# Issuing the fallback path's DMAs from GpSimd in place of SyncE, in a fused ReGLU MLP

## The chip, the cores and the metric

The kernel runs on one core of one Trainium2 chip. The metric is the device time of one execution in microseconds (us). "Ratio" always means the mean time of one kernel's fast runs over the mean time of the other kernel's fast runs measured beside them, without the profiled run, so it is not quite the ratio of the medians that are quoted beside it. A run counts as fast when it is at most 1.5% above the fastest of the same kernel; all timed runs here were fast, and the one run that was looked at only once counts as of unknown state.

## The reference

```python
batch, seq, dim, hidden = 16, 256, 512, 2048
# x: (16, 256, 512), w1: (512, 4096), w2: (2048, 512), all drawn from a normal distribution, float32
def reference(x, w1, w2):
    h = x @ w1
    gate, value = np.split(h, 2, axis=-1)
    h = np.maximum(gate, 0) * value
    return (h @ w2).astype(np.float32)
```

## The kernel before

The kernel holds two ways of computing the result. The fast way works in float16 with fewer products (a Strassen scheme), and while it runs it checks that the inputs' sizes allow this. The check ends in one number, `flag`. If the flag is set, a general way computes everything again in float32. For the inputs the flag is never set: the general way is in the program, but none of its instructions runs.

```python
def tile_reglu_mlp_kernel(ctx, tc, x, w1, w2, out):
    ...
    with ExitStack() as fast:
        unfit = fast_way(fast, tc, x2, w1, w2, out2, flag)
    with tc.If(unfit > 0, label="general"):
        with ExitStack() as general:
            general_way(general, tc, x2, w1, w2, out2)

def general_way(ctx, tc, x2, w1, w2, out2):
    ...
    for k in range(NK):
        for j in range(0, 2 * H, 1024):
            t = xp.tile([P, 1024], F32, name="g_t", tag="g_t")
            nc.sync.dma_start(out=t, in_=w1[k * P:(k + 1) * P, j:j + 1024])
            nc.vector.tensor_copy(out=w1_sb[:, k, j:j + 1024], in_=t)
    ...                      # 16 loads of w1, 16 of w2, 32 of x, 32 stores: 96 DMAs, all from SyncE

# in the fast way: the last output of all
        def P4(self):
            nc.scalar.activation(self.o[:, 1, :DO // 2], self.Y, COPY, scale=1 / GS)
            self.send(1, slice(0, DO // 2 if self.end else DO))       # SyncE issues it
# ... and the flag, read into a register of each of the five engines 11 to 19 us before the end
            job(78, lambda: verdict.append(nc.values_load(flag[0:1, 0:1], ...)))
            job(84, lambda: tc.mark_branch_hint_location("general", "LikelyTaken", [ENG.PE, ENG.DVE, ENG.SP]))
```

What the author doesn't write, the framework adds. Every DMA from SyncE adds 16 to one of eight semaphores ("lanes"), in turn; DMAs from GpSimd have eight lanes of their own. (To issue a DMA is to hand a transfer to the DMA engines; it has landed when its last part of 16 has been counted.) At the very end SyncE waits until all lanes and all engines' counters stand at their final values. A final value must be the same whichever arm of the `If` ran. So the empty arm has to raise every lane by what the general way would have added, and it may do that only when the lane's own last DMA has landed. This is SyncE's built program after its last output DMA, which is on lane 7:

```
branch on the register
empty arm:  8 x   wait until lane i >= 208, then add 192 to lane i          (i = 0 ... 7)
end:        3 x   wait for two GpSimd lanes each
            8 x   wait until lane i >= 400 (and for one engine's counter)   (i = 0 ... 7)
            drain, drain, barrier, GpSimd clears the semaphores, barrier
```

## Time and profile before

Six runs gave a median of 309.47 us (308.88 to 310.2); the first three of them gave 309.0 us. The first lines below are from the page of the profiled execution: each engine's busy time with its share of the span, and the chain of work that ended last.

```profile
span 307.5 us, 5285 instructions
...
PE 300.7 (98%) x1905; PEld 184.0 (60%) x1905; DVE 235.9 (77%) x388; ACT 176.4 (57%) x348; POOL 151.4 (49%) x189
...
## 4 chain that ended last, share of the span: by engine, by line
PE 96%; DMA 1%; SPq 0%; POOL 0%; ACT 0%; issue 0%
```

TensorE (PE) is busy for 98% of the span and makes up 96% of the chain. A change elsewhere can help only at the two ends. The end is where this one acts. Next come lines of three views of the same execution: SyncE's timeline (start in us, duration in us, what), the view of the source line of the `If` (L42), and that of the end of the program (L785). "SPq" is SyncE's sequencer; the three numbers before the times are the least, median and largest duration in ns.

```profile
303.38 1.07 SPq L370 DMA_DIRECT2D out_dram<-o  x1
```

```profile
L42 SPq EVENT_SEMAPHORE  x8: 17/17/17, 305.0 to 305.8; - x8
...
L42 SPq COMPARE_BRANCH  x1: 73/73/73, 304.5 to 304.5; - x1
```

```profile
L785 SPq EVENT_SEMAPHORE  x13: 17/28/28, 305.9 to 307.4; - x13
```

They read as a queue in order: the last output is issued from 303.38 on, SyncE branches at 304.5, eight semaphore instructions of the empty arm run from 305.0 to 305.8, and only after the eighth do the end waits begin. (Eleven of the 13 instructions on L785 are the end waits; the last two belong to the barriers.) With one digit more, from the records of the single instructions and of the DMA's semaphore updates:

| event | us |
|---|---|
| ScalarE's last eviction (the copy of the last result out of TensorE's accumulator) ends | 303.353 |
| SyncE issues the last output | 303.379 to 304.451 |
| SyncE branches | 304.502 to 304.575 |
| adds on lanes 0 to 6 | 305.030 to 305.522 |
| last part of the last output lands | 305.814 |
| add on lane 7 | 305.831 |
| eleven end waits | 305.897 to 306.544 |
| end of the span | 307.461 |

From the landing to the end it is 1.647 us. The last issue takes 1.07 us although most output issues take 0.33, and after SyncE's branch 0.455 us pass before its next record.

### The profile page before, as it was taken

How to read it: one execution, taken by the hardware profiler on the slowest of the kernel's cores; microseconds unless marked ns; L12 is line 12 of the kernel's file. 1: busy time of each engine (PE TensorE's matmuls, PEld its weight loads, DVE VectorE, ACT ScalarE, POOL GpSimd, SP SyncE). 2: the span in 40 equal slices, each digit the busy share in tenths (PEclk: the TensorE clock that was granted, in tenths of full speed). 3: DMA queues.
4: the chain of work that ended last, by engine and by line, in shares of the span. 5: the costliest groups of instructions: out<-in, count | busy, mean ns of one | idle time of the engine just before them, and what ended most of it. 6: DMA issues, size and time to landing. Idle time of an engine off the chain costs nothing.

```text
span 307.5 us, 5285 instructions
## 1 busy us (share of the span) xinstructions
PE 300.7 (98%) x1905; PEld 184.0 (60%) x1905; DVE 235.9 (77%) x388; ACT 176.4 (57%) x348; POOL 151.4 (49%) x189
## 2 busy tenths in 40 slices
PE   7999999999999999999999999999999999999994
PEld 6844444588844444478864444458884444448883
DVE  2579888899768888887438888889536888888841
ACT  2488886455865555538845555546865555553231
POOL 2389999800069899200029889700007998700000
PEclk9999999999999999999999999999999999999998
DMA  6976779964765260001354910000335110001132
GB/s 207 357 257 190 227 177 174 225 123 87 270 193 86 69 136 3 0 0 67 136 175 103 207 34 2 0 2 24 115 108 167 35 34 0 3 1 34 53 120 74
DMA packets 35837, 32.88 MB, mean 107 GB/s; under 512 B 14432, under 2 KB 31328, under 8 KB 35680
## 3 DMA queue, kind: packets, MB, share of 16 engines
q1 hardware_dynamic: 33536, 26.22, 28.0%
q0 software_dynamic: 2272, 6.29, 11.4%
q8 instruction: 16, 0.26, 0.4%
q14 instruction: 13, 0.11, 0.1%
HBM read 27.26 MB, written 12.58 MB: 130 GB/s over the span
## 4 chain that ended last, share of the span: by engine, by line
PE 96%; DMA 1%; SPq 0%; POOL 0%; ACT 0%; issue 0%
PE Y L250 26%; PE X L250 17%; PE W L250 17%; PE Y L362 14%; PE X L362 9%; PE W L362 9%; DMA w_stage<-in_w_dram 1%; PE X L325 1%; PE W L325 1%; PE Y L325 1%; PE Y L498 0%; PE X L498 0%; SPq L488 0%; PE Y L154 0%; POOL w_B L466 0%; ACT o L405 0%
## 5 line engine op out<-in xcount | busy, mean ns | idle before, releaser
L250 PEld LDWEIGHTS <-w_T 128*128 128x128 f16 x496 | 48.3, 98 | 57.3 <-POOL w_T L232 1.1
L179 POOL TENSOR_TENSOR fold<-xh 128x1024 f32<-128x1024 f16 x16 | 30.3, 1894 | 94.5 <-DMA xh<-x 93.7
L250 PE MATMUL X<-x_A,w_B 128*128 128x512 f16 x248 | 73.8, 379 | 0.0
L250 PE MATMUL Y<-x_S,w_T 128*128 128x512 f16 x220 | 65.5, 379 | 0.0
L250 PEld LDWEIGHTS <-w_B 128*128 128x128 f16 x372 | 36.4, 98 | 42.0
L277 DVE SCALAR_TENSOR_TENSOR cc<-W,pu 128x512 f32<-128x512 f32 x62 | 42.9, 691 | 21.2 <-ACT pu L271 20.4
L257 ACT COPY Y<-X 128x512 f32<-128x512 f32 x62 | 35.4, 571 | 38.2 <-PE X L250 37.9
L271 ACT ACTIVATE pu<-Y 128x512 f32<-128x512 f32 x62 | 37.1, 598 | 33.9 <-PE Y L250 32.9
L182 POOL TENSOR_TENSOR fold<-fold 128x512 f32<-128x512 f32 (+2 forms) x96 | 51.8, 539 | 7.5
L362 PEld LDWEIGHTS <-w_stage 128*128 128x128 f16 x512 | 50.0, 98 | 5.8
L287 DVE SCALAR_TENSOR_TENSOR cc<-Y,pu 128x512 f32<-128x512 f32 x62 | 42.9, 691 | 6.7
L282 DVE SCALAR_TENSOR_TENSOR g<-X,cc 128x512 f16<-128x512 f32 x62 | 42.8, 691 | 2.3
L299 DVE SCALAR_TENSOR_TENSOR g<-Y,cc 128x512 f16<-128x512 f32 x62 | 42.2, 681 | 1.8 <-PE Y L250 1.8
L362 PEld LDWEIGHTS <-g 128*128 128x128 f16 x384 | 37.6, 98 | 8.2
L264 ACT ACTIVATE pu<-W 128x512 f32<-128x512 f32 x62 | 37.2, 600 | 0.8 <-PE W L250 0.6
L250 PE MATMUL W<-x_S,w_B 128*128 128x512 f16 x124 | 36.9, 379 | 0.0
L250 PE MATMUL W<-x_S,w_T 128*128 128x512 f16 x124 | 36.9, 379 | 0.0
L250 PE MATMUL Y<-x_A,w_T 128*128 128x512 f16 x124 | 36.9, 379 | 0.0
L362 PE MATMUL X<-w,g 128*128 128x256 f16 x256 | 31.9, 273 | 0.0
L394 DVE SCALAR_TENSOR_TENSOR o<-W,pu 128x256 f32<-128x256 f32 x16 | 6.8, 422 | 19.8 <-PE W L362 19.8
L169 DVE TENSOR_TENSOR w_stage<-g 128x1024 f16<-128x1024 f16 x32 | 21.4, 683 | 0.2
L232 POOL TENSOR_TENSOR w_T<-w_stage 128x512 f16<-128x512 f32 (+1 forms) x16 | 18.7, 1177 | 2.5 <-DMA w_stage<-in_w_dram 2.5
(100 smaller groups left out, 306.2 us busy)
## 6 DMA issues: line engine op xcount, KB each, us to landing
w_stage<-in_w_dram SPq DMA_DIRECT2D x14, 512.0 KB, 6.2
out_dram<-o SPq DMA_DIRECT2D x26, 256.0 KB, 2.1
x<-in_x_dram POOLq DMA_DIRECT2D x4, 1024.0 KB, 9.0
xh<-x SPq DMA_DIRECT2D x16, 256.0 KB, 3.0
w<-in_w_dram POOLq DMA_DIRECT2D x2, 1024.0 KB, 10.2
out_dram<-o SPq DMA_DIRECT2D x12, 128.0 KB, 1.7
w_stage<-in_w_dram SPq DMA_DIRECT2D x4, 256.0 KB, 5.4
x_S<-in_x_dram SPq DMA_DIRECT2D x4, 256.0 KB, 6.1
```

The lines of the kernel that those rows point to most:

```text
L169: eng.tensor_tensor(o[n], o[i0], o[i1], op=op)
L179: nc.gpsimd.tensor_tensor(fold, t, t, op=MULT)
L182: nc.gpsimd.tensor_tensor(fold[:, :, :m], fold[:, :, :m], fold[:, :, m:2 * m], op=ADD)
L250: nc.tensor.matmul(ps, wop[wn][:, b, self.jb * P:(self.jb + 1) * P], self.xo[xn][:, b, :], start=fresh and b == 0, stop=b == 1, skip_group ...
L257: nc.scalar.copy(out=self.Y, in_=self.X)
L264: nc.scalar.activation(self.p5, self.W, COPY, scale=GS)
L271: nc.scalar.activation(self.u2, self.Y, COPY, scale=GS)
L277: nc.vector.scalar_tensor_tensor(out=self.c12, in0=self.W, scalar=GS, in1=self.u2, op0=MULT, op1=ADD)
L282: nc.vector.scalar_tensor_tensor(out=self.g[:, self.jb, :TH], in0=self.X, scalar=0.0, in1=self.c12, op0=MAX, op1=MULT)
L287: nc.vector.scalar_tensor_tensor(out=self.c22, in0=self.Y, scalar=GS, in1=self.p5, op0=MULT, op1=ADD)
L299: nc.vector.scalar_tensor_tensor(out=self.g[:, self.jb, TH:], in0=self.Y, scalar=0.0, in1=self.c22, op0=MAX, op1=MULT)
L362: nc.tensor.matmul(ps, self.op[an][:, i], vop[wn][:, i], start=name in ("P1", "P5") and i == 0, stop=i == NJ // 2 - 1, skip_group_check=True)
```

## The change

The general way issues its DMAs from GpSimd. The intent is in the change's own words: no SyncE lane has then to be balanced between the two arms.

```diff
@@ general_way: all four DMA lines (loads of w1, w2, x; store of the output)
-            nc.sync.dma_start(out=t, in_=w1[k * P:(k + 1) * P, j:j + 1024])
+            nc.gpsimd.dma_start(out=t, in_=w1[k * P:(k + 1) * P, j:j + 1024])
 ...
-            nc.sync.dma_start(out=out2[c * TH + b * P:c * TH + (b + 1) * P, :], in_=o)
+            nc.gpsimd.dma_start(out=out2[c * TH + b * P:c * TH + (b + 1) * P, :], in_=o)
```

In the built program, the instructions of all five engines up to the branch are the same, waits included. SyncE's empty arm has nothing left to do. GpSimd's empty arm gets four waits for GpSimd lanes and one increment of the eight of them, which waits too (the view of L42 below counts five waits, because one was there before). There are twelve end waits, since all eight GpSimd lanes are used now.

More of the change, by code (lines that the diff above doesn't have):

```diff
@@ L66, in general_way @@
         t = xp.tile([P, DO], F32, name="g_t", tag="g_t")
-        nc.sync.dma_start(out=t, in_=w2[h * P:(h + 1) * P, :])
+        nc.gpsimd.dma_start(out=t, in_=w2[h * P:(h + 1) * P, :])
         nc.vector.tensor_copy(out=w2_sb[:, h], in_=t)
@@ L72, in general_way @@
             t = xp.tile([P, D], F32, name="g_t", tag="g_t")
-            nc.sync.dma_start(out=t, in_=x2[c * TH + b * P:c * TH + (b + 1) * P, :])
+            nc.gpsimd.dma_start(out=t, in_=x2[c * TH + b * P:c * TH + (b + 1) * P, :])
             for k in range(NK):
```

## The prediction

> **What bounds the kernel.** TensorE: the page gives PE 98% busy at clock 0.996, and the chain that ended last is 96% PE, up to 302.95 of the 307.46 us span. The general way does not run for this input: none of its instructions is in the trace. So the change acts only after the flag's test, in the last 3 us. Up to the branch, all engines' instruction order is unchanged.
>
> **The tail before, from the instruction records of the last 5 us.** The last ScalarE eviction ends at 303.35. SyncE issues the last output DMA at 303.379 (1.07 us; most issues take 0.33), branches at 304.502 (73 ns) and has its next record at 305.030: the empty arm, eight waits-and-adds, one for each SyncE lane, that raise it by the 192 counts which the general way would have added. Seven take 80 ns each (305.03 to 305.52); the eighth waits for the last DMA, landed at 305.814, and runs at 305.831. Then come eleven end waits, 62 ns each (305.897 to 306.544), two drains, barrier, semaphore clear, second barrier; the span ends at 307.46, 0.945 us after the last end wait began.
>
> **What the change removes and adds.**
> - SyncE: the eight adds go, so the end waits start right after the branch. They are twelve now. Eleven ask for what is long done: started between 304.65 and 305.0, they are over by 305.35 to 305.7, behind the flight of the last DMA. The twelfth passes with its landing, about 305.83.
> - So ten end waits leave the chain: landing, one wait, the same 0.945 us. Estimate: end at 306.78, 0.68 us earlier.
> - SyncE's branch goes over one instruction in place of about 190. The Trainium skill ("Runtime: NRT & Kernel Launch", Instruction fetch mechanics) says that a taken branch to a target outside the fetched window forces a fetch. The trace agrees in kind: 0.455 us from SyncE's branch to its next record, 0.13 us on ScalarE, whose general arm is empty. This 0.3 us helps only what is hidden.
> - GpSimd: five waits and one increment of software DMA semaphores are added, and its branch gets longer. It branches at 289.48 and is needed at 306.68; 2 us is hidden.
> - PE, DVE, ACT: unchanged.
>
> **Prediction.** 309.0 − 0.7 = 308.3 us, range 307.5 to 309.2. Chances: faster by over 2% 0.01, within 2% 0.98, slower by over 2% 0.01.
>
> **What would show each step right.**
> - Instruction records: no SyncE adds after its branch; first end wait within 0.2 us of the branch's end; eleven over before the last landing, the twelfth within 30 ns of it; from landing to the end of the span about 0.96 us, where it was 1.65.
> - Page: PE's busy time, the chain and the DMA counts unchanged; a few more GpSimd instructions, all near 290 us.
> - The landing stays near 305.8 if the 1.07 us issue stays. It ran beside two instruction fetches (16 KB from 303.06, 8 KB from 303.60), which look like PE's and SyncE's.
>
> **What would make it wrong.** If the 8 KB fetch belongs to SyncE's far jump and slows the last issue, it may vanish: up to 0.7 us more (307.6). If SyncE has to stop for a fetch within its end waits, part of the gain is lost. 0.2% is near the spread of single runs (308.88 to 310.2), so the medians may hide it. Over 2 us would mean that something before the branch moved.

## The result, and the profile after

| | before | after |
|---|---|---|
| median of 6 runs, us | 309.47 (308.88 to 310.2) | 308.38 (307.95 to 309.21) |
| ratio, 95% interval | | 0.997 [0.995, 0.999] |
| span of the profiled run, us | 307.461 | 307.156 |

In a later set of five rounds the changed kernel gave 308.44 us against 309.2 us, ratio 0.9983 [0.9968, 0.9997]. So the gain is 0.2 to 0.3%, some 0.5 to 0.9 us. By the rule of 2% this is "the same"; the intervals exclude no gain at all.

These are the lines of the changed kernel's profile that answer to the ones above, from the page, from SyncE's timeline, and from the views of L42 and L785 (POOL is GpSimd).

```profile
span 307.2 us, 5283 instructions
...
PE 301.6 (98%) x1905; PEld 184.2 (60%) x1905; DVE 236.0 (77%) x388; ACT 176.3 (57%) x348; POOL 151.2 (49%) x189
...
PE 96%; DMA 2%; SPq 1%; issue 0%; ACT 0%
```

```profile
303.48 1.34 SPq L370 DMA_DIRECT2D out_dram<-o  x1
```

```profile
L42 POOLq EVENT_SEMAPHORE  x5: 17/43/43, 290.1 to 290.4; - x5
...
L42 POOLq INC_SWDGE_SEM  x1: 316/316/316, 290.5 to 290.5; - x1
...
L42 SPq COMPARE_BRANCH  x1: 68/68/68, 304.9 to 304.9; - x1
```

```profile
L785 SPq EVENT_SEMAPHORE  x14: 17/28/28, 305.1 to 307.1; - x14
```

The eight SyncE instructions on L42 are gone, and the end waits begin 0.137 us after the branch. GpSimd's new work (1.2 us from the end of its branch to the end of the increment) is over at 290.8, 14 us before SyncE's first end wait asks for it (305.08). The waits of SyncE (engine and line that waited, for what, total us, times, longest) show the same thing from the other side, first before the change, then after it, both from 303 us on:

```profile
SPq L42 <- SPq L42: 0.8, 2, 0.5
SPq L785 <- PEq L785: 0.7, 2, 0.5
```

```profile
SPq L785 <- PEq L785: 0.7, 2, 0.5
SPq L785 <- DMA out_dram<-o: 0.4, 1, 0.4
```

Before, SyncE waited on L42 (the empty arm); the profile puts these two waits down to SyncE itself, but the second of them (305.522 to 305.831 in the records) ended with the landing at 305.814. After, the one wait for the output DMA is an end wait, the twelfth and last one: it passes at 306.210, 0.017 us after the landing at 306.193. The eleven others were over at 305.746. From the landing to the end it is 0.963 us, 0.684 less than before.

The profiled span fell by 0.305 us only, because the landing came later: ScalarE's last eviction ended 0.098 us later, and the last issue took 1.344 us in place of 1.072. That second number isn't the change's doing, as the experiments show; it moves from run to run.

### The profile page after: what moved, and what is told of

Its sections match the earlier page's. It is cut to its first block, busy times and chain, and to the rows that moved or that the text cites. A ratio compares the mean times of both kernels' runs of the same rounds, so it can differ in the third digit from the quotient of the medians.

```text
span 307.2 us, 5283 instructions
## 1 busy us (share of the span) xinstructions
PE 301.6 (98%) x1905; PEld 184.2 (60%) x1905; DVE 236.0 (77%) x388; ACT 176.3 (57%) x348; POOL 151.2 (49%) x189
## 2 busy tenths in 40 slices
DMA packets 35836, 32.87 MB, mean 107 GB/s; under 512 B 14432, under 2 KB 31328, under 8 KB 35680
## 4 chain that ended last, share of the span: by engine, by line
PE 96%; DMA 2%; SPq 1%; issue 0%; ACT 0%
PE Y L250 26%; PE X L250 17%; PE W L250 17%; PE Y L362 14%; PE W L362 9%; PE X L362 9%; DMA x_A<-in_x_dram 2%; PE X L325 1%; PE W L325 1%; PE Y L325 1%; PE Y L498 0%; PE X L498 0%; SPq L217 0%; SPq L488 0%; ACT o L405 0%
```

## The experiments

ScalarE's last eviction ends anywhere from 302.6 to 303.5 us in the profiled runs, with the same program before it. This spread is as large as the effects. So the table measures each run's profile from there: the last output's issue, its flight from the end of the issue to the last landing, and the stretch from the landing to the end. Together with some 0.03 us before the issue they make up the tail. Each row rests on one profile, but the stretch from the landing to the end repeats closely: it is 0.963 or 0.964 us in all eight profiles in which SyncE has a branch and no adds, and 1.647 in both with the full adds of the kernel before. All in us; median and ratio as above.

| run | last issue | flight | landing to end | tail | median | ratio to the kernel before |
|---|---|---|---|---|---|---|
| before | 1.072 | 1.363 | 1.647 | 4.108 | 309.47 | 1 |
| changed kernel | 1.344 | 1.371 | 0.963 | 3.705 | 308.38 | 0.997 [0.995, 0.999] |
| e1: 8 loads on SyncE | 1.215 | 1.372 | 1.710 | 4.322 | 309.51 | 1.002 [0.9998, 1.0042] |
| e2: 7 loads on SyncE | 1.376 | 1.365 | 1.381 | 4.148 | 308.95 | 0.9996 [0.998, 1.0013] |
| e3: far jump | 0.992 | 1.378 | 0.963 | 3.358 | 308.31 | 0.9979 [0.9962, 0.9995] |
| e4: no general way | 0.332 | 1.359 | 0.958 | 2.674 | 307.65 | 0.9961 [0.9943, 0.9979] |
| e5: late branch | 0.333 | 1.369 | 0.964 | 2.692 | 307.62 | 0.995 [0.9933, 0.9966] |
| e6: late PE only | 0.332 | 1.598 | 0.963 | 2.918 | 307.79 | 0.9964 [0.9942, 0.9985] |
| e7: late DVE only | 1.038 | 2.119 | 0.964 | 4.146 | one look | |
| e8: ScalarE sends | 0.376 | 2.236 | 0.964 | 3.606 | 308.37 | 0.9976 [0.9953, 0.9999] |
| e9: before, late branch | 0.332 | 1.365 | 1.647 | 3.369 | 308.33 | 0.9974 [0.9961, 0.9987] |
| e10: changed kernel again | 1.210 | 1.369 | 0.964 | 3.568 | 308.44 | 0.9983 [0.9968, 0.9997] |
| e11: late branch again | 0.332 | 1.365 | 0.964 | 2.686 | 307.72 | 0.9957 [0.9944, 0.997] |

The runs e1 to e4 shared one set of runs of the kernel before (308.84 us), e5 to e8 another (309.06), e9 to e11 a third (309.2). All results were correct.

### Is it the adds, or the shorter program?

The change does two things to SyncE: it takes the eight adds out of the empty arm, and it shortens SyncE's program, so that the branch no longer jumps over some 190 instructions. Theory A says that the add on lane 7 is the cost: it waits for the last landing and stands, in order, in front of all end waits. Rival B says that the long jump is the cost.

**e1** puts eight loads of the general way back on SyncE, one for each lane.

```diff
-            nc.gpsimd.dma_start(out=t, in_=w1[k * P:(k + 1) * P, j:j + 1024])
+            eng = nc.sync if k * 4 + j // 1024 < 8 else nc.gpsimd
+            eng.dma_start(out=t, in_=w1[k * P:(k + 1) * P, j:j + 1024])
```

> The changed kernel, with the first 8 loads of the general way back on SyncE: one for each of its eight lanes, so the empty arm has eight adds of 16 again, among them the add on lane 7, which the last output DMA uses. SyncE's jump stays short (about 25 instructions). Theory A (an add on the lane of the last DMA stands in order before the end waits and holds all twelve back until the landing): no gain; from the last landing to the end of the span 1.71 us (1.65 as before, one end wait of 0.06 more), time near the kernel before (ratio 0.998 to 1.002). Rival B (the gain comes from the shorter SyncE program and jump): landing to end 0.96 us and ratio about 0.997.

The views of L42 and of the program's end, in e1:

```profile
L42 SPq EVENT_SEMAPHORE  x8: 17/17/17, 305.1 to 305.9; - x8
```

```profile
L786 SPq EVENT_SEMAPHORE  x14: 17/28/28, 306.0 to 307.5; - x14
```

The stretch from the landing to the end is 1.710 us, as Theory A had it to the last digit, and the gain in time is gone (ratio 1.002). But the test was less clean than planned. After SyncE's branch 0.455 us pass before the next record, as in the kernel before, not 0.137 as after the change; in that sense 25 instructions were already a long jump. So e1 alone doesn't refute Rival B.

**e2** has seven loads there, so only the add on lane 7 goes (`< 7` in the same line).

> As the run before, but 7 loads on SyncE: the empty arm has seven adds, on lanes 0 to 6, none on lane 7. One DMA less than the run before, in an arm that never runs. Theory A: seven adds (0.08 us each) and eleven end waits (0.062 us each) can run while the last DMA flies; they need 1.25 us from SyncE's branch, and the landing comes about 1.3 us after it, so landing to end is 0.96 to 1.2 us: 0.5 to 0.75 less than with eight. Rival B: the same as with eight, to 0.06 us.

The same two views, in e2:

```profile
L42 SPq EVENT_SEMAPHORE  x7: 17/17/17, 305.0 to 305.4; - x7
```

```profile
L786 SPq EVENT_SEMAPHORE  x14: 17/28/28, 305.5 to 307.1; - x14
```

The end waits start at 305.494, before the landing at 305.738; in e1 they started after it. One DMA less, in an arm that never runs, takes 0.329 us out of the stretch after the landing. It did not reach the expected 0.96 to 1.2 us, and the miss is arithmetic: I had counted with a gap of 0.14 us after the branch, and it was 0.456. The branch ended at 304.496; 0.456 of gap, seven adds in 0.54 and eleven end waits in 0.68 us take SyncE to 306.17. So the twelfth wait came 0.435 us after the landing: now SyncE's own queue was the last to finish. In time e2 can't be told from the kernel before (0.9996, with 1 inside the interval), so what it shows is in its trace alone.

**e3** leaves SyncE without adds, but makes its program as long as before, with 190 drains (a sequencer instruction, filler here) in the arm that never runs.

```diff
     make_identity(nc, ident)
+    for _ in range(190):
+        nc.sync.drain()
```

> The changed kernel, with 190 drains put into SyncE's general arm, which never run: no adds in the empty arm, but SyncE's program is as long and its jump as far as before the change. Theory A: landing to end stays at 0.96 us; after the branch there is a gap of some 0.45 us (0.14 with the short jump), hidden behind the landing up to about 0.2 us of it at most not. Rival B: the gain goes, landing to end near 1.65 us, ratio about 1.000.

The same two views, in e3, where SyncE has only its branch on L42:

```profile
L42 SPq COMPARE_BRANCH  x1: 73/73/73, 304.5 to 304.5; - x1
```

```profile
L787 SPq EVENT_SEMAPHORE  x14: 17/28/28, 305.0 to 306.7; - x14
```

The jump is far again (gap 0.455 us, and the branch takes 73 ns as before the change, not 68), and the gain stays whole: 0.963 us from the landing to the end, ratio 0.9979. Rival B falls. The far jump does cost 0.32 us, but on an engine that then waits for the landing anyway.

### What makes the last issue slow?

With the adds gone, the tail still has an issue of 1.0 to 1.4 us where 0.33 is usual. In both first traces a 16 KB instruction fetch of PE overlaps it. PE branches at 301.79 (before), jumps far, and 0.77 us after the branch's end a fetch begins. These are DMA records, on queue 8 for PE and queue 14 for the other engines (start and end, in us; e7 and e10 came later):

| run | PE's fetch (16 KB) | last issue | issue's end after the fetch's |
|---|---|---|---|
| before | 303.057 to 304.071 | 303.379 to 304.451 | 0.380 |
| changed kernel | 303.151 to 304.442 | 303.478 to 304.822 | 0.380 |
| e1 | 302.962 to 304.128 | 303.294 to 304.509 | 0.381 |
| e2 | 302.666 to 303.992 | 302.997 to 304.373 | 0.381 |
| e3 | 303.148 to 304.139 | 303.467 to 304.459 | 0.320 |
| e7 | 302.943 to 303.938 | 303.273 to 304.311 | 0.373 |
| e10 | 302.544 to 303.708 | 302.879 to 304.089 | 0.381 |

In six of the seven the issue ends 0.37 to 0.38 us after the fetch does; in e3 0.32. That pointed to Theory C, that PE's fetch holds up the issue, against Rival D, that the last issue is slow for a reason of its own.

**e4** leaves the general way out (right for these inputs only), and with it the branch and the jumps.

```diff
-    with tc.If(unfit > 0, label="general"):
-        with ExitStack() as general:
-            general_way(general, tc, x2, w1, w2, out2)
...
-            job(84, lambda: tc.mark_branch_hint_location("general", "LikelyTaken", [ENG.PE, ENG.DVE, ENG.SP]))
```

> The changed kernel without the general way, the branch and its hints (right for these inputs only): a floor, and a test of what slows the last output's issue. In both traces the 16 KB instruction fetch of PE that begins 0.8 us after PE's branch overlaps that issue, and the issue ends 0.38 us after the fetch. Theory C (PE's fetch holds the issue up): without the jump there is no such fetch, the last issue takes 0.33 us and its landing comes 0.7 to 1.0 us earlier; with that the span falls by about 0.8 us against the changed kernel (ratio to the kernel before about 0.994). Rival D (the last issue is slow for a reason of its own): it still takes over 1 us.

SyncE's timeline and its waits in e4:

```profile
303.16 0.33 SPq L367 DMA_DIRECT2D out_dram<-o  x1
```

```profile
SPq L781 <- DMA out_dram<-o: 0.7, 1, 0.7
```

There is no fetch after 299.43 us, and the last issue takes 0.332 us. The tail is 1.03 us shorter than the changed kernel's. The ratio is 0.9961 where about 0.994 was expected, and its interval, [0.9943, 0.9979], just misses that. But e4 takes away too much to name the cause, hence the next runs.

**e5** keeps everything and only moves the fetches: PE and DVE must wait for a ScalarE copy after the last eviction before they branch. The result of the read isn't used; the framework keeps of it a plain wait on ScalarE's counter.

```diff
         prev = stream
+    late = wpool.tile([1, 1], dt.int32, name="late")
+    nc.scalar.copy(out=late, in_=flag)
+    nc.values_load(late[0:1, 0:1], engines=(ENG.PE, ENG.DVE), min_val=0, max_val=1,
+                   skip_runtime_bounds_check_because="a copy of the flag")
     return verdict[-1]
```

> The changed kernel, with PE and DVE kept from their branches until ScalarE has copied the flag after its last eviction, so that the instruction fetches which follow their jumps (about 0.8 us after PE's, 1.4 us after DVE's) begin near 304.9 us in place of 303.1 and 303.7, when the last output has nearly landed. Theory C (a fetch that runs beside the last issue holds it up): the last issue takes 0.33 us, its landing comes about 1.4 us after the end of the issue, near 304.9, and the span is about 0.6 to 1.2 us shorter than that of the changed kernel (ratio to the kernel before 0.993 to 0.996). Rival D (the issue is slow for a reason of its own): it still takes over 0.9 us, and the ratio stays near 0.997 to 0.998.

From e5, SyncE's timeline and the view of L42:

```profile
303.15 0.33 SPq L370 DMA_DIRECT2D out_dram<-o  x1
```

```profile
L42 DVEq COMPARE_BRANCH  x1: 90/90/90, 303.3 to 303.3; - x1
L42 PEldq COMPARE_BRANCH  x1: 497/497/497, 303.4 to 303.4; - x1
L42 SPq COMPARE_BRANCH  x1: 68/68/68, 303.5 to 303.5; - x1
```

PE and DVE now branch at 303.4 and 303.3, 1.5 and 1.1 us later than in the changed kernel. Their fetches begin at 304.614 and 304.744, somewhat earlier than I expected, but still after the last output's data had been moved (its last packet ended at 304.506). The last issue takes 0.333 us, and the tail is 2.692 us: that of e4, with the general way in place. Rival D falls. The ratio is 0.995 [0.9933, 0.9966], and 0.9957 [0.9944, 0.997] when the run was repeated.

**e6 and e7** hold back only PE (`engines=(ENG.PE,)`) or only DVE (`engines=(ENG.DVE,)`).

> As the run before, but only PE waits; DVE jumps early, and its 8 KB fetch falls into the last issue. If it is PE's 16 KB fetch that holds the issue up: 0.33 us again, but one of the 16 parts of the last or the last but one output may land up to 1 us late, so the gain may be partly lost. If any fetch does: about 0.8 us of issue (the 8 KB fetch ends near 304.05, and 0.38 us more).

> As that, but only DVE waits; PE's 16 KB fetch falls into the last issue as in the changed kernel. Theory C with PE's fetch as the cause: the issue takes 1.0 to 1.35 us and ends 0.38 us after that fetch; of the last but one output only one of 16 parts lands late, not two. If DVE's fetch is the cause: 0.33 us.

The last issue in e6 and in e7, from SyncE's timelines:

```profile
302.99 0.33 SPq L370 DMA_DIRECT2D out_dram<-o  x1
```

```profile
303.27 1.04 SPq L370 DMA_DIRECT2D out_dram<-o  x1
```

In e7 PE's fetch (302.943 to 303.938) alone gives an issue of 1.038 us, and one part of the last but one output is late, not two, as expected; so PE's fetch is enough. In e6 DVE's fetch (303.082 to 303.609) alone leaves it at 0.332; but it began 0.1 us after the issue did, so this doesn't show that an 8 KB fetch could never do harm. What each fetch does to a transfer is plain in the landings of the single parts. An output lands in 16 parts, which normally arrive within 0.2 us. The parts of the last but one output and the last one:

| run | fetches beside it | last but one output | last output |
|---|---|---|---|
| changed kernel | PE's and DVE's | 14 by 304.35; 305.21, 305.63 | 16 from 306.01 to 306.19 |
| e5 | none | 16 by 304.02 | 16 from 304.68 to 304.86 |
| e6 | DVE's (303.08), PE's (304.47) | 15 by 303.86; 304.61 | 15 by 304.68; 304.92 |
| e7 | PE's (302.94), DVE's (304.99) | 15 by 304.14; 305.11 | 15 by 305.69; 306.43 |

Each fetch that ran while an output's packets moved made one of its 16 parts late, by 0.2 to 1.3 us against the slowest of the others. (In e6 PE's fetch began only 0.01 us before the last data packet ended, so the late part of the last output is more likely DVE's doing.) The same happens far from the end: in all 13 traces PE's fetches near 153, 219 and 298 us also left one part of an output late, by 0.8 to 1.7 us. A fetch is one DMA record, and one part in sixteen is one DMA engine's share. The Trainium skill ("DMA: Bandwidth & Descriptors", Queues, rings and completion order) says that a queue has a ring on each of 16 engines, and that each engine takes turns between the rings it has work for. The records fit: in the changed kernel all packets of the last but one output had started by 303.99 but for 18, two shares of nine, which ran from 304.111 to 305.15, as DVE's fetch (to 304.115) and PE's (to 304.442) ended; and the DMA counts as landed only with its last part. The records kept here don't name the engine of a packet, so that the late shares sit on the fetches' engines is inferred.

**e8** lets ScalarE issue the last output in place of SyncE.

```diff
-            self.send(1, slice(0, DO // 2 if self.end else DO))
+            self.send(1, slice(0, DO // 2 if self.end else DO), nc.scalar if self.end and self.t == 3 else nc.sync)
...
-        def send(self, h, c):
-            nc.sync.dma_start(out=out_v[self.s, h, self.t, :, c], in_=self.o[:, h, c])
+        def send(self, h, c, eng=nc.sync):
+            eng.dma_start(out=out_v[self.s, h, self.t, :, c], in_=self.o[:, h, c])
```

> The changed kernel, with the very last output issued by ScalarE, which made its data, in place of SyncE. If PE's fetch holds up any issue through the shared DMA engines: ScalarE's issue also ends about 0.38 us after the fetch, and the span does not change by more than 0.2 us. If the hold-up is one of SyncE's own sequencer or queue: ScalarE's issue takes about 0.33 us, and the landing comes 0.7 us or more earlier.

ScalarE's timeline and the list of DMA issues (count, KB, us from issue to landing) in e8:

```profile
303.32 0.38 ACTq L370 DMA_DIRECT2D out_dram<-o  x1
```

```profile
out_dram<-o ACTq DMA_DIRECT2D x1, 128.0 KB, 2.6
```

Neither alternative was right as a whole. The issue takes 0.376 us, though PE's fetch (302.983 to 304.431) runs all through it: a fetch does not hold up every issue beside it. Yet little is won, since two of the 16 parts still land late (305.43 and 305.94; the other 14 by 305.04), and the flight is 2.236 us. So the faster issue alone brought nothing: the tail of 3.606 us lies between those of the changed kernel's two profiles (3.705 and 3.568). The Trainium skill says in the same page (Issuing engines are not separate DMA queues) that using several issuing engines saves only the time of the issue; this run agrees so far as only the issue got shorter, and even of these 0.97 us 0.87 were lost again in the flight, against the changed kernel's first profile.

Why SyncE's issue is held and ScalarE's isn't stays open. SyncE still had its last but one output in flight, with a part stuck behind the fetch; ScalarE had nothing. Much fits "an issue waits while SyncE's own previous DMA is stuck behind the fetch": over the 13 traces SyncE issued 20 outputs while a fetch of PE was running, and 19 of them took 0.72 to 1.41 us and ended 0.32 to 0.38 us after the fetch, each with an earlier output of SyncE's in flight that had a late part. In the kernel before, the output at 299.013, beside the fetch of 298.371 to 299.652, took 1.018 us. In e4, which has no branch at all, one at 298.794 took 1.012, so it needs no jump, only a fetch of PE. But two observations speak against the rule as it stands. The twentieth output, in e1 at 298.927, took 0.333 us, although the output before it (issued at 298.054) was in flight and had one part that landed only at 301.317, 1.2 us after the others; that issue began 0.034 us after its fetch (298.893 to 299.825), the held ones at least 0.32 us. And in the kernel before, a load issued at 36.804, inside PE's fetch of 36.172 to 37.297, took 0.367 us with an earlier load of SyncE's still in flight; only the next one was held. No run took one condition away by itself, so the reason is not shown.

### Are the two costs separate?

**e9** puts the late branch of e5 on the kernel before; **e10** and **e11** repeat the changed kernel and e5 beside it.

> The kernel before, with PE's and DVE's branches held until after the last eviction as in the run of the late branch. If the two costs are separate, only the landing moves: last issue 0.33 us, landing about 1.37 us after its end, but landing to end 1.65 us as before the change (the add on lane 7 is in front of the end waits again); span about 306.5 us, 0.68 us over the late branch on top of the change; ratio to the kernel before about 0.997.

> The changed kernel itself, to have it in the same rounds as its two neighbours: landing to end 0.96 us, last issue 1.0 to 1.35 us, ratio 0.997 to 0.998.

> The late branch on top of the change, in the same rounds as the changed kernel: landing to end 0.96 us, last issue 0.33 us, span 0.6 to 1.2 us under the changed kernel's, ratio to the kernel before 0.993 to 0.996.

SyncE's lines in e9, from its timeline and the view of L42:

```profile
303.10 0.33 SPq L370 DMA_DIRECT2D out_dram<-o  x1
```

```profile
L42 SPq EVENT_SEMAPHORE  x8: 17/17/17, 304.0 to 304.8; - x8
```

The last issue is short, and the adds cost as before: 1.647 us from the landing to the end. The tails are 3.369 (e9) and 2.686 us (e11), and the difference of 0.683 us is what the change is worth with the fetches out of the way; with them in the way it was 1.647 − 0.963 = 0.684. The costs are separate and add up. In time, the change alone, the late branch alone and both together give the ratios 0.9983, 0.9974 and 0.9957, so the two savings of 0.17% and 0.26% sum to 0.43%, which is what both give. That the sum is exact is luck, for each ratio is known only to some 0.13%; it is the tails that show the sum.

The best kernel is therefore the changed one with the late branch (e5, e11): 307.62 and 307.72 us, 0.43 to 0.5% under the kernel before. Its interval in the last set, [0.9944, 0.997], touches that of the changed kernel, [0.9968, 0.9997], only at its edge; its tail is 0.9 to 1.0 us shorter. The margin is thin: the first fetch began 0.108 us after the last output's last data packet had ended in e5, but only 0.008 us after it in e11.

## Why the prediction was right

- **Where the change acts.** Right. All instructions up to the branch are the same, PE's share of the chain stays at 96%, the DMA packets at 35,837 and 35,836, and all of the gain is after the landing of the last output.
- **The size.** Right: 0.68 us from the landing to the end was worked out, 0.684 measured, and e1, e3 and e9 took it away, kept it, and found it again on another base. Predicted 308.3 us, measured 308.38. This closeness is partly luck: the kernel before came out at 309.0 in the first runs and at 309.47 in all six, so the measured difference is 1.09 us, and 0.76 in the later set. The tail, not the medians, confirms the 0.68.
- **The mechanism.** Right: no adds after the branch, the first end wait 0.137 us after the branch's end (under 0.2 expected), eleven waits over 0.45 us before the landing, the twelfth within 0.02 us of it.
- **The shorter jump helps only what is hidden.** Right, and e3 shows it. e2 shows the limit: with seven adds left, the longer gap did come out into the open.
- **GpSimd's new work is hidden.** Right: 1.2 us near 290 us, from four new waits, where five were forecast, and the increment.
- **The landing stays near 305.8 if the 1.07 us issue stays.** Half right. The issue stayed slow, but its length follows PE's fetch (0.99 to 1.38 us in these runs), so it was 1.34 us and the landing came at 306.19. This took 0.27 us from the profiled gain.
- **Whose the fetches are.** PE's was named rightly. The 8 KB fetch "from 303.60" was said to look like SyncE's; it is DVE's. It moves with DVE's branch in e5 and e7 (to 304.74 and 304.99), stays in e6, and is there in the changed kernel, whose SyncE jumps short. The fetch that SyncE's far jump caused is a later one, at 305.58 before; it is missing after the change and is back in e3 at 305.59, and it delayed nothing.

What stays open: no run used inputs for which the general way runs, so what the change does to that way's own time is not known. Nor is it shown why the last eviction's end moves by up to 0.9 us between profiles (by 0.6 us between the two of the changed kernel), or why a fetch of PE holds up an issue of SyncE's and not one of ScalarE's.

## What to carry to other kernels

Code that never runs can cost time where it is joined to the code that does: look at what each arm of a branch must do to leave the semaphores equal, and keep any such step that has to wait for the last transfer out of the last engine's queue, or on an engine that is done early. The last output of a kernel is also a bad moment for other engines to jump far (here it cost 0.9 to 1.0 us): hold their jumps back until the data has moved, with a wait that cost nothing here because these engines were idle by then. When effects are a fraction of a percent, measure the stretch of the trace in which they act, from one fixed event to the next, and use the medians only to check the sum.

## What the Trainium skill lacked or had wrong

- "Runtime: NRT & Kernel Launch" (Instruction fetch mechanics) says that a taken branch to a target outside the fetched window forces a fetch before execution goes on, and calls the cost of crossing a block mostly hidden. These runs agree with a cost on the engine itself (SyncE's gap after a far jump is 0.455 us against 0.137), but the larger cost is on others, which the page lacks: a 16 KB fetch of PE held up SyncE's last issue by 0.7 to 1.0 us, and each fetch that ran while an output's packets moved made one of its 16 parts 0.2 to 1.7 us late. In the kernel before, on PE and SyncE, a recorded fetch came 0.77 and 1.0 us after the far jump's end, when the first instructions at the target had already run.
- The same section gives refill blocks of 16 KiB. In these traces PE's fetches are 16,384 bytes, but those of the other engines are 8,192; whether that is a setting of the runtime or a property of the chip, the runs can't tell.
- "DMA: Bandwidth & Descriptors" (Issuing engines are not separate DMA queues) does not say that an issue itself can be held up by other traffic, and differently by engine: beside PE's fetch, SyncE's last issue took 0.99 to 1.38 us and ScalarE's 0.376.
- "Advanced Engine Details and Errata" (Control Flow Timing) gives about 108 ns for a compare-and-branch. Here it took 45 ns on GpSimd, 50 to 54 on ScalarE, 68 to 73 on SyncE, 90 on DVE, and 408 to 501 on PE.
- No page tells what an empty arm costs: eight semaphore waits-and-adds of about 80 ns each on SyncE, and end waits of about 62 ns each, in order.
